# Copying mLSTM scores out of PSUM at once, and loading the low-rank matrices as 128 rows, in a hybrid mixer layer

## The chip, the cores and the metric

The kernel runs on one core of a Trainium2 chip. The metric is the time of one execution on the device in microseconds; lower is better. The core has a matrix engine (TensorE, "PE" in the profile, with its weight loads as "PEld"), three engines for elementwise work (VectorE or DVE, ScalarE or ACT, GpSimd or POOL), a sync engine (SyncE or SP) that issues most transfers, and 16 DMA engines that carry them. Matmuls write to PSUM, a small memory of eight banks of 128 x 512 fp32 numbers; everything else lies in SBUF, 128 partitions wide.

## What is computed

The reference is one layer of a trunk with four parallel token mixers (a convolution module, a bidirectional mLSTM, a bidirectional gated DeltaNet, a bidirectional RWKV-7) on 256 context and 256 latent tokens of width 2048, merged with sigmoid gates, and then a gated convolutional feed-forward. Two places matter here. The mLSTM scan, for each of four heads and two directions:

```python
s = jnp.einsum('ghtd,ghsd->ghts', qt, kt) * dw
num = iw[..., None] * jnp.einsum('ghtd,ghde->ghte', qt, C) + jnp.einsum('ghts,ghse->ghte', s, vt)
den = iw * jnp.einsum('ghtd,ghd->ght', qt, n) + jnp.sum(s, axis=-1)
h = num / jnp.maximum(jnp.abs(den), jnp.exp(-mt))[..., None]
```

and the low-rank decay and learning-rate projections of RWKV-7, of rank 96 plus one bias row:

```python
wl = p['rw_w0'] + jnp.einsum('btr,nrw->btnw', jnp.tanh(xw), p['rw_w2'])
iclr = jax.nn.sigmoid(p['rw_a0'] + jnp.einsum('btr,nrw->btnw', xa, p['rw_a2']))
```

## The kernel before

**Large products.** Every large weight matrix is streamed once. `load_split` (L187 to L200) loads 256 rows as two tiles of 128 rows (`raw`, four buffers, issued by SyncE at L194), makes a rounded high part on ScalarE (`hi`, L198) and the rest on VectorE (`lo`, L199), two buffers each; TensorE then does three products for each block (high by high, high by low, low by high), all at L79. `mode_b_steps` keeps the weights as the stationary operand (`psB`), `mode_a` the tokens (`psA`).

**Order of the work.** The program is written stage by stage: modulation and first projections (`phase0`), the RWKV columns, features and scan, the columns of the other branches, the DeltaNet scan, the mLSTM scan (`ml_scan`), the gate columns (`gates`), the end of the convolution module, the four merges (branches 3, 2, 1, 0), the output projection, the feed-forward. The order in which each engine takes its instructions isn't that of the text: the program is built with `schedule_with_timeline_sim=True`, so a planner simulates it and orders each engine's queue, and matmuls of the gates stand between those of the mLSTM scan. On the chip each engine then works strictly in its queue's order. Tiles get their SBUF addresses from the pools, and a tile that takes over the place of another waits until that one was read for the last time. A generator feeds pieces of the modulation product (`psw`, `psf`) in between.

**The low-rank load.** `rw_open` makes the tile `lora` of 97 partitions, 2 x 2 x 512 numbers each, and `rw_columns` fills it with one transfer (L578) from an input that `layout` puts together on the host (96 rank rows and the bias row). The same function starts the product with `w_mix` (eight loads of 480 KB), whose loads stand behind it in SyncE's queue. `rw_feat` reads `lora` in 32 matmuls (`pslo`).

**The mLSTM scan.** `ml_scan` treats all 512 keys and the 256 latent queries of a head at once. It takes its PSUM banks from a pool of three ("aux"). For each head, eight matmuls write the scores to two banks (`psq0`, `psq1`). Then for each direction d: five matmuls write the row terms of the decay logarithm, with the mask, to one bank (`psr`); ScalarE makes the weights `mA` by exponentials (L1248, L1251, L1253); VectorE multiplies them with the scores in PSUM (L1255, L1256, L1259); fourteen matmuls with the values write numerator and denominator to one bank (`psn`); ScalarE and VectorE normalise into `mlh` (L1267 to L1274). `mA` has two buffers. The masks are drawn by GpSimd in a tile `mlmf` and copied to bf16 by VectorE (L1235), ahead of the heads. After the heads, `head_out` normalises `mlh` over heads and writes the branch's output for its merge.

**The merge.** `merge` loads gate values (`sig`, issued at L1332) and multiplies them with the product of a branch (L1338 for the first merge, L1340 after that).

Of the kernel before, what the change touches and what calls it, by code (L numbers as in the profile page):

```python
# [11 lines left out]
F32 = mybir.dt.float32  # L12
# [8 lines left out]
P = 128  # L21
# [20 lines left out]
class Kern:  # L42
# [499 lines left out]
    def rw_open(self):  # L542
        rp = self.pool("rp2", stack=self.rwx, side="right")
        T = lambda nm, s: rp.tile(s, F32, name=nm)
        self.kT, self.kk = T("kT", [P, 4, 512]), T("kk", [P, 4, 512])
        self.thx, self.xa, self.g32 = T("thx", [97, 512]), T("xa", [97, 512]), T("g32", [32, 512])
        self.rT, self.vL = T("rT", [P, 4, 256]), T("vL", [P, 4, 256])
        self.lora = T("lora", [97, 2, 2, 512])
        self.w2, self.a2 = self.lora[:, 0], self.lora[:, 1]
        self.dv = self.dp.tile([512, 4, P], F32, name="dv")  # L550

    def rw_columns(self):
# [623 lines left out]
    def ml_scan(self):  # L1176
        nc = self.nc
        self.mlx = ExitStack()
        mp = self.pool("mrp", stack=self.mlx)
        wa = self.pool("mwa", bufs=2, stack=self.mlx)  # L1180
        wp = self.pool("mwb", bufs=2, stack=self.mlx)
        qk = self.pool("mqk", stack=self.mlx)
        mqT, mkT = qk.tile([P, 4, 256], F32, name="mqT"), qk.tile([P, 4, 512], F32, name="mkT")
        mv = mp.tile([P, 4, 4, 132], F32, name="mv")
        nc.gpsimd.memset(mv[:, :, :, 128:129], 1.0)
        nc.sync.dma_start(out=mqT, in_=self.dmq)
        nc.sync.dma_start(out=mkT, in_=self.dmk)
        for j in range(4):
            nc.sync.dma_start(out=mv[:, j, :, 0:P], in_=self.dmv[:, j].rearrange("p (h e) -> p h e", h=4))
        e = mp.tile([P, 4, 2, 4], F32, name="mle")  # L1190
        em = mp.tile([P, 2, 2, 4], F32, name="mlem")
        rr = []
        ident = self.ident
        for d in range(2):
            li, lf, b, m = (mp.tile([4, 512], F32, tag="mr%d" % k, name="mr%d" % k) for k in range(4))
            for src, dst in ((self.li, li), (self.lf, lf)):
                ps = self.aux("psml")
                for j in range(4):
                    self.tr(ps[0:4, P * j : P * j + P], src[:, j, d])
                nc.scalar.activation(dst, ps[0:4], AF.Copy)  # L1200
            one = self.ones[0:4, 0:1].to_broadcast([4, 256])
            for seg in range(2):
                v = (lambda ap: ap[:, 0:256] if seg == 0 else ap[:, 256:512])
                f = v if d == 0 else (lambda ap: ap[:, 255::-1] if seg == 0 else ap[:, 511:255:-1])
                pos = 255 if d == 0 else 0
                i0 = (0.0, 0.0) if seg == 0 else (b[:, pos : pos + 1], m[:, pos : pos + 1])
                nc.vector.tensor_tensor_scan(f(b), one, f(lf), i0[0], ALU.mult, ALU.add)
                nc.vector.tensor_tensor_scan(f(m), f(lf), f(li), i0[1], ALU.add, ALU.max)
            nc.vector.tensor_tensor(li, li, b, ALU.subtract)
            ps = self.aux("psmt")  # L1210
            for j in range(4):
                self.tr(ps[:, 4 * j : 4 * j + 4], li[:, P * j : P * j + P])
            for j in range(2):
                self.tr(ps[:, 16 + 4 * j : 20 + 4 * j], m[:, 256 + P * j : 384 + P * j])
            nc.vector.tensor_copy(e[:, :, d], ps[:, 0:16].rearrange("p (j h) -> p j h", h=4))
            nc.scalar.activation(em[:, :, d], ps[:, 16:24].rearrange("p (j h) -> p j h", h=4), AF.Exp, scale=-1.0)
            self.dbg("mlm%d" % d, m)
            self.dbg("mlb%d" % d, b)
            r = mp.tile([4, 256], F32, name="mlr%d" % d)
            nc.vector.tensor_tensor(r, b[:, 256:512], m[:, 256:512], ALU.subtract)  # L1220
            rr.append(r)
        sel = mp.tile([4, 4, P], F32, name="mlsel")
        for h in range(4):
            nc.vector.tensor_copy(sel[:, h], ident[0:4, h : h + 1].to_broadcast([4, P]))
        idb = mp.tile([P, P], BF16, name="idb")
        nc.vector.tensor_copy(idb, ident)

        ms = mp.tile([P, 2, 2, P], BF16, name="mlmask")
        mf = mp.tile([P, P], F32, name="mlmf")
        for d in range(2):  # L1230
            nc.gpsimd.memset(mf, 0.0)
            sg = 1 if d == 0 else -1
            nc.gpsimd.affine_select(out=mf, in_=mf, pattern=[[sg, P]], compare_op=ALU.is_ge, fill=-1e30, base=0, channel_multiplier=-sg)
            for i in range(2):
                nc.vector.tensor_copy(ms[:, d, i], mf)  # L1235
        hs = mp.tile([P, 2, 4, P], F32, name="mlh")
        for h in range(4):
            pq = [self.aux("psq%d" % i) for i in range(2)]
            for j in range(4):
                self.mm(pq[j // 2][:, 256 * (j % 2) : 256 * (j % 2) + 256], mkT[:, h, P * j : P * j + P], mqT[:, h])  # L1240
            for d in range(2):
                pr = self.aux("psr")
                self.mm(pr[:, 0:256], sel[:, h], rr[d])
                self.mm(pr[:, 256:512], sel[:, h], rr[d], start=True, stop=False)
                self.mm(pr[:, 256:512], idb, ms[:, d].rearrange("p i t -> p (i t)"), start=False, stop=True)
                A = wa.tile([P, 4, 256], F32, tag="mA", name="mA")
                for j in range(2):
                    nc.scalar.activation(A[:, j], pr[:, 0:256], AF.Exp, bias=e[:, j, d, h : h + 1])  # L1248
                full = (2, 1) if d == 0 else (3, 0)
                bl = lambda i: slice(P * i, P * i + P)  # L1250
                nc.scalar.activation(A[:, full[0], bl(full[1])], pr[:, bl(full[1])], AF.Exp, bias=e[:, full[0], d, h : h + 1])  # L1251
                for i in range(2):
                    nc.scalar.activation(A[:, 2 + i, bl(i)], pr[:, 256 + P * i : 384 + P * i], AF.Exp, bias=e[:, 2 + i, d, h : h + 1])  # L1253
                A2 = lambda ap: ap.rearrange("p j t -> p (j t)")
                nc.vector.tensor_tensor(A2(A[:, 0:2]), A2(A[:, 0:2]), pq[0], ALU.mult)  # L1255
                nc.vector.tensor_tensor(A[:, full[0]], A[:, full[0]], pq[1][:, 256 * (full[0] - 2) : 256 * (full[0] - 2) + 256], ALU.mult)  # L1256
                o = 5 - full[0]
                ob = bl(o - 2)
                nc.vector.tensor_tensor(A[:, o, ob], A[:, o, ob], pq[1][:, 256 * (o - 2) + ob.start : 256 * (o - 2) + ob.stop], ALU.mult)  # L1259
                pn = self.aux("psn")  # L1260
                for i in range(2):
                    js = [j for j in range(4) if j < 3 or i == 1] if d == 0 else [j for j in range(4) if j != 2 or i == 0]
                    for q, j in enumerate(js):
                        self.mm(pn[:, 132 * i : 132 * i + 129], A[:, j, bl(i)], mv[:, j, h, 0:129], start=q == 0, stop=q == len(js) - 1)
                dn = wp.tile([P, 2, 1], F32, tag="dn", name="dn")
                p3 = pn[:, 0:264].rearrange("p (i c) -> p i c", c=132)
                nc.scalar.activation(dn, p3[:, :, 128:129], AF.Abs)  # L1267
                nc.vector.tensor_tensor(dn, dn, em[:, :, d, h : h + 1], ALU.max)
                nc.vector.reciprocal(dn, dn)
                for i in range(2):  # L1270
                    if d == 0:
                        nc.vector.tensor_scalar(hs[:, i, h], p3[:, i, 0:P], dn[:, i], None, ALU.mult)
                    else:
                        nc.vector.scalar_tensor_tensor(hs[:, i, h], p3[:, i, 0:P], dn[:, i], hs[:, i, h], ALU.mult, ALU.add)  # L1274
        self.dbg("mlh", hs)
        self.head_out(mp, "mh", hs, self.mo, "ml_norm_g", 1)
        self.mlx.close()
# [369 lines left out]
def layout(inputs):  # L1647
# [27 lines left out]
    lora = [np.concatenate([f[w][0].transpose(1, 0, 2), f[b][0][None]], axis=0) for w, b in (("rw_w2", "rw_w0"), ("rw_a2", "rw_a0"))]  # L1675
    r = {n: f[n] for n in ("x", "ctx", "w_mod", "b_mod", "norm_g", "w_in", "rw_g2", "w_br", "w_out", "ffn_up", "ffn_down")}
    r["vec"] = np.concatenate([cols[nm] for nm in VEC], axis=1)
    r["lora"] = np.stack(lora, axis=1)
    r["w_mix"] = np.concatenate([wi[:, C_XW : C_XW + 96], wi[:, C_MLG : C_MLG + 16], wi[:, C_GDG : C_GDG + 16], wi[:, C_XA : C_XA + 352]], axis=1)
    r["taps"] = f["ffn_dw"][0].reshape(396, P).T  # L1680
    return {n: np.ascontiguousarray(a) for n, a in r.items()}
# [18 lines left out]
```

## Time and profile before

| | us |
|---|---|
| three runs | 2306.84, 2308.45, 2312.79 (median 2308.45) |
| profiled execution, its own time | 2311.59 |
| its span, first to last instruction | 2309.5 |
| TensorE busy | 2209.9 |
| VectorE busy | 1446.7 |
| ScalarE busy | 994.1 |
| GpSimd busy | 364.4 |
| mean granted TensorE clock | 0.982 of full speed |

The profile is that of one execution. Busy time is the time in which an engine ran an instruction; the granted clock is the share of TensorE's full speed that the chip allowed at the time. Tiles are named as in the program, without buffer numbers. A wait is put down to the instruction that ended it. A row of the timeline gives start and length in microseconds, engine, line, operation, output and inputs, and in brackets the idle time ahead of it with what ended it.

### The profile page before, as it was taken

The numbers are of one execution on the slowest core, as the hardware profiler recorded it, in microseconds if no ns is written. First come the engines' busy times: TensorE is split into PE (matmuls) and PEld (weight loads), VectorE is DVE, ScalarE is ACT, GpSimd is POOL, SyncE is SP. The second block draws the span as 40 slices with busy tenths as digits, with TensorE's granted clock in tenths as the row PEclk, the third lists the DMA queues.
The fourth block names the chain that finished last, engine by engine and source line by source line (L and its number), as shares of the span: only waits on it lengthen the run. The fifth ranks groups of instructions, "written<-read, shape, count | busy, mean of one in ns | idle before, by whom it ended". The sixth has DMA issues, their size and how long they took to land.

```text
span 2309.5 us, 42812 instructions
## 1 busy us (share of the span) xinstructions
PE 2209.9 (96%) x16828; PEld 1807.2 (78%) x16828; DVE 1446.7 (63%) x3084; ACT 994.1 (43%) x1506; POOL 364.4 (16%) x736
## 2 busy tenths in 40 slices
PE   6979899999999999999999899989999999999998
PEld 3657667877888677677777678779999999998886
DVE  3357766734555698457564486568766677775554
ACT  4225644533444344344245344454333344444443
POOL 0012553533455021010000033000000000000000
PEclk8989999999999999999999899999999999999999
DMA  9934663555665777777786576567777666666663
GB/s 371 361 111 127 171 185 113 161 172 158 198 201 172 242 231 244 235 236 215 215 265 209 172 264 205 174 208 228 229 222 226 210 183 183 176 212 201 194 193 101
DMA packets 273867, 471.97 MB, mean 204 GB/s; under 512 B 41761, under 2 KB 80929, under 8 KB 272673
## 3 DMA queue, kind: packets, MB, share of 16 engines
q1 hardware_dynamic: 273378, 467.14, 65.2%
q8 instruction: 132, 2.16, 0.4%
q10 hardware_dynamic: 288, 2.10, 0.2%
q14 instruction: 69, 0.57, 0.1%
HBM read 440.33 MB, written 28.84 MB: 203 GB/s over the span
## 4 chain that ended last, share of the span: by engine, by line
PE 83%; DVE 7%; DMA 5%; ACT 3%; issue 2%; POOL 1%; SPq 0%; DVEq 0%; ACTq 0%; POOLq 0%
PE psB L79 37%; PE psA L79 21%; PE psD L79 10%; PE psw L79 4%; DVE lo L199 2%; DMA wraw<-in_w_mod 2%; DMA raw<-in_w_mix 1%; PE psG L79 1%; ACT hi L198 1%; DVE cacc L869 1%; PE psf L79 1%; PE psn L79 1%; DMA raw<-in_w_in 1%; PE psSA L79 1%; PE psY L79 0%
## 5 line engine op out<-in xcount | busy, mean ns | idle before, releaser
L199 DVE TENSOR_TENSOR lo<-raw,hi 128x1024 fp32r<-128x1024 f32 (+2 forms) x488 | 600.9, 1233 | 452.9 <-ACT hi L198 443.4
L198 ACT ACTIVATE hi<-raw 128x1024 fp32r<-128x1024 f32 (+2 forms) x488 | 508.4, 1044 | 792.6 <-PE psB L79 347.3
L79 PE MATMUL psB<-u2l,hi 128*128 128x256 f32 x1408 | 396.3, 283 | 0.0
L79 PE MATMUL psB<-u2h,lo 128*128 128x256 f32 x1408 | 395.8, 284 | 0.0
L79 PE MATMUL psB<-u2h,hi 128*128 128x256 f32 x1408 | 394.1, 286 | 0.0
L79 PE MATMUL psA<-lo,uh 128*128 128x512 f32 x832 | 336.7, 405 | 8.9 <-DVE lo L199 8.7
L79 PE MATMUL psA<-hi,ul 128*128 128x512 f32 x832 | 331.1, 398 | 0.0
L79 PE MATMUL psA<-hi,uh 128*128 128x512 f32 x832 | 310.7, 404 | 4.5 <-DVE mg L1338 3.5
L79 PE MATMUL psB<-uh,hi 128*128 128x256 f32 (+1 forms) x832 | 279.7, 344 | 18.6 <-ACT hi L198 16.3
L79 PE MATMUL psB<-ul,hi 128*128 128x256 f32 (+2 forms) x832 | 278.6, 339 | 0.0
L79 PEld LDWEIGHTS psB<-u2h,hi 128*128 128x128 f32 x1408 | 266.9, 192 | 10.4 <-issue 10.3
L79 PE MATMUL psB<-uh,lo 128*128 128x256 f32 (+2 forms) x832 | 263.0, 339 | 8.1 <-DVE lo L199 8.1
L79 PEld LDWEIGHTS psB<-u2l,hi 128*128 128x128 f32 x1408 | 270.7, 192 | 0.0
L79 PEld LDWEIGHTS psB<-u2h,lo 128*128 128x128 f32 x1408 | 269.9, 192 | 0.5 <-issue 0.4
L79 PEld LDWEIGHTS psA<-lo,uh 128*128 128x128 f32 x832 | 157.4, 189 | 59.4 <-DVE lo L199 16.1
L79 PEld LDWEIGHTS psB<-uh,hi 128*128 128x128 f32 x832 | 157.9, 190 | 50.5 <-ACT hi L198 18.4
L79 PEld LDWEIGHTS psA<-hi,uh 128*128 128x128 f32 x832 | 154.6, 190 | 52.9 <-issue 14.1
L79 PEld LDWEIGHTS psA<-hi,ul 128*128 128x128 f32 x832 | 157.3, 189 | 35.7 <-issue 2.0
L79 PEld LDWEIGHTS psB<-uh,lo 128*128 128x128 f32 (+1 forms) x832 | 152.9, 189 | 32.0 <-DVE lo L199 10.6
L79 PEld LDWEIGHTS psB<-ul,hi 128*128 128x128 f32 (+1 forms) x832 | 157.8, 190 | 22.8 <-issue 6.2
L1550 DVE TENSOR_TENSOR lo<-raw,hi 128x1024 fp32r<-128x1024 f32 x88 | 107.6, 1225 | 77.1 <-ACT hi L1549 77.0
L1457 DVE SCALAR_TENSOR_TENSOR facc<-fpad,ffdw,facc 128x256 f32<-128x256 f32 x352 | 151.1, 483 | 0.2
(570 smaller groups left out, 2879.6 us busy)
## 6 DMA issues: line engine op xcount, KB each, us to landing
raw<-in_w_in SPq DMA_DIRECT2D x208, 512.0 KB, 4.5
raw<-in_ffn_up SPq DMA_DIRECT2D x176, 512.0 KB, 3.8
wraw<-in_w_mod SPq DMA_DIRECT2D x160, 512.0 KB, 5.3
raw<-in_ffn_down SPq DMA_DIRECT2D x88, 512.0 KB, 4.4
raw<-in_w_br SPq DMA_DIRECT2D x32, 512.0 KB, 4.8
raw<-in_w_out SPq DMA_DIRECT2D x32, 512.0 KB, 4.7
raw<-in_w_mod SPq DMA_DIRECT2D x32, 512.0 KB, 4.7
raw<-in_w_in SPq DMA_DIRECT2D x48, 256.0 KB, 4.1
```

Of the source, the lines that this page charges most:

```text
L79: self.nc.tensor.matmul(out, lhsT, rhs, start=start, stop=stop)
L198: nc.scalar.activation(hi[s], raw[s], AF.Copy)
L199: nc.vector.tensor_tensor(lo[s], raw[s], hi[s].bitcast(F32), ALU.subtract)
L869: nc.vector.scalar_tensor_tensor(a, cpad[:, i, t : t + 256], w(i, t), a, ALU.mult, ALU.add)
L1457: nc.vector.scalar_tensor_tensor(s3(acc), pad[:, dy : dy + 4, dx : dx + 64], tap(t, b), s3(acc), ALU.mult, ALU.add)
L1550: nc.vector.tensor_tensor(f(lo), f(raw), f(hi).bitcast(F32), ALU.subtract)
```

## The change

Three edits. The tile `lora` gets 128 partitions instead of 97, and the host pads the input with zeros to 128 rows; the matmuls read the first 97 as before. In `ml_scan`, both score banks are copied to an SBUF tile `sc` of one buffer, one by VectorE and one by ScalarE, and the products with the weights read `sc`. The mask is drawn in a corner of the result tile `mlh`, which is made earlier for that, and the tile `mlmf` is gone.

```diff
-        self.lora = T("lora", [97, 2, 2, 512])
-        self.w2, self.a2 = self.lora[:, 0], self.lora[:, 1]
+        self.lora = T("lora", [P, 2, 2, 512])
+        self.w2, self.a2 = self.lora[0:97, 0], self.lora[0:97, 1]
...
-        mf = mp.tile([P, P], F32, name="mlmf")
+        hs = mp.tile([P, 2, 4, P], F32, name="mlh")
+        mf = hs[:, 0, 0]
...
-        hs = mp.tile([P, 2, 4, P], F32, name="mlh")
         for h in range(4):
             pq = [self.aux("psq%d" % i) for i in range(2)]
             for j in range(4):
                 self.mm(pq[j // 2][:, 256 * (j % 2) : 256 * (j % 2) + 256], mkT[:, h, P * j : P * j + P], mqT[:, h])
+
+            sc = mp.tile([P, 2, 512], F32, tag="sc", name="msc")
+            for i in range(2):
+                self.evac(sc[:, i], pq[i], "act" if i else "dve")
+            pq = [sc[:, i] for i in range(2)]
...
-    r["lora"] = np.stack(lora, axis=1)
+
+    r["lora"] = np.pad(np.stack(lora, axis=1), ((0, P - 97), (0, 0), (0, 0), (0, 0)))
```

## The prediction

> **What bounds the kernel now.** The page comes first: who is busy, and where that breaks off.
>
> ```profile
> PE 2209.9 (96%) x16828; PEld 1807.2 (78%) x16828; DVE 1446.7 (63%) x3084; ACT 994.1 (43%) x1506; POOL 364.4 (16%) x736
> PE   6979899999999999999999899989999999999998
> PEclk8989999999999999999999899999999999999999
> PE 83%; DVE 7%; DMA 5%; ACT 3%; issue 2%; POOL 1%; SPq 0%; DVEq 0%; ACTq 0%; POOLq 0%
> ```
>
> TensorE (PE) is busy for 96% of the span, and 83% of the chain that ended last is its work. Work that TensorE covers is free; a microsecond is won only where TensorE stands still or runs at a low clock. Both edits lie beside such places. The granted clock drops to 0.8 in the third slice (115 to 173 us, which holds several small gaps) and again in the 23rd (1270 to 1328); to find the exact stretches I cut the span into stages.
>
> ```profile
> core 0: us, PE busy (x) PEld busy (x) DVE busy (x) ACT busy (x) POOL busy (x), PEclk, DMA share, GB/s
> 161.70:173.20 11.50, 0.00 (x0) 0.00 (x0) 2.68 (x1) 1.00 (x1) 2.62 (x3) 0.61 0.20 64
> 173.20:178.00 4.80, 4.76 (x11) 3.23 (x12) 2.32 (x2) 1.09 (x2) 0.00 (x0) 0.50 0.53 142
> 1207.00:1298.00 91.00, 91.00 (x488) 67.04 (x486) 40.73 (x68) 46.83 (x73) 1.31 (x1) 1.00 0.69 209
> 1298.00:1303.40 5.40, 4.28 (x21) 2.89 (x17) 1.27 (x2) 2.14 (x5) 0.00 (x0) 1.00 0.59 190
> 1303.40:1320.40 17.00, 9.71 (x45) 7.68 (x45) 6.23 (x18) 2.87 (x11) 2.82 (x3) 0.63 0.26 72
> 1320.40:1325.00 4.60, 4.54 (x11) 3.57 (x12) 3.77 (x13) 0.00 (x0) 0.53 (x1) 0.51 0.84 320
> 1360.00:1380.00 20.00, 17.83 (x75) 13.66 (x74) 14.93 (x13) 6.37 (x6) 8.63 (x7) 1.00 1.00 382
> ```
>
> Columns: length, busy time (count) by engine, granted clock, DMA share, GB/s. From 161.7 to 173.2 TensorE does nothing, and it then works 4.8 us at clock 0.50. From 1207 to 1298 it is full at clock 1.00; from 1298 to 1325 it has gaps and a low clock. One hole follows the low-rank load, the other is the end of the mLSTM scan.
>
> **First hole: the low-rank load.** The timeline of SyncE (SPq), the listing of transfers by stretch, and the waits around it:
>
> ```profile
> lora<-in_lora SPq DMA_DIRECT2D x1, 776.0 KB
> 135.83 0.31 SPq L578 DMA_DIRECT2D lora<-in_lora  x1
> 143.88 32.16 SPq L194 DMA_DIRECT2D raw<-in_w_mix  x6
> 135.90:143.80 7.90, 7.90 (x34) 6.40 (x32) 3.94 (x8) 2.26 (x3) 0.27 (x4) 0.93 0.07 23
> raw<-in_w_mix SPq DMA_DIRECT2D x2, 480.0 KB, 28.5
> raw<-in_w_mix SPq DMA_DIRECT2D x8, 480.0 KB, 4.3
> mkT<-dmk SPq DMA_DIRECT2D x1, 1024.0 KB, 7.5
> 172.19 1.00 ACT L198 ACTIVATE hi<-raw 128x960 fp32r<-128x960 f32 x1 [11.20 <-DMA raw<-in_w_mix]
> 173.24 0.79 PE L79 MATMUL psB<-uh,hi 128*128 128x512 f32 x1 [11.59 <-ACT hi L198]
> 178.06 0.39 PE L79 MATMUL psB<-uh,hi 128*128 128x512 f32 x1
> L79 PE MATMUL pslo<-thx,lora x16: 590/592/697, 207.4 to 296.6; 97*128 97x512 f32 x16
> 160.29 0.69 ACT L516 ACTIVATE rwsq<-pskk,eps 128x512 f32<-128x512 f32 x1 [5.93 <-PE pskk L79]
> 161.04 3.34 DVE L517 RECIPROCAL rwsq<-rwsq 128x512 f32<-128x512 f32 x1
> 191.19 1.14 DVE L199 TENSOR_TENSOR lo<-raw,hi 128x960 fp32r<-128x960 f32 x1
> ```
>
> The load of 97 rows goes out at 135.83. Until 143.8 nothing else of weight is moved, and the 16 DMA engines show a share of 0.07 and 23 GB/s: about one of sixteen works. At 23 GB/s 776 KB take 34.5 us, so it ends near 170. The w_mix loads issued from 143.88 on have a share on that same engine, queue behind it there, and land after 28.5 us where their median is 4.3. ScalarE's split (L198) waits 11.20 us for that and TensorE 11.59 us for the split.
>
> With 128 rows the load has the row count of mkT, which is as large (1024 KB) and lands in 7.5 us: it is in by 143.4, ahead of the w_mix loads. Its first reader starts at 207.4, so the extra 248 KB cost nothing; if that cover were gone they would cost 248 KB at 382 GB/s (the rate of the stretch 1360 to 1380), 0.7 us. Then the w_mix data lie ready at about 149. With each queue's order as it is, ScalarE ends its square root at 160.98 and the split at 161.99, 0.3 us after TensorE's last matmul. TensorE then has eight matmuls on the high part and two pskk, which at full clock take half of the 3.6 us that they took at clock 0.50 (173.24 to 176.88), so 1.8 plus start, and is at the low part by 164.3 at the latest; VectorE is in a reciprocal until 164.38 and needs 1.14 us more for the low part, so TensorE waits for 1.2 us. Gain: 11.5 idle, plus half of 4.76 us that ran at clock 0.50, 2.4, less 0.3 and 1.2: **12.4 us**, of which I take 12. What is late next is that reciprocal. Bounds: 14 if the planner moves the low part ahead of it; 9 if the w_mix loads, or VectorE, bring 3 us of new gaps. Everything behind 178 hangs on this chain and moves up with it.
>
> **Second hole: the end of the mLSTM scan.** Timelines of the last head, and the waits of SyncE:
>
> ```profile
> 1295.57 1.89 PE L79 MATMUL psq<-mqT,mkT 128*128 128x256 f32 x8
> 1300.94 1.13 PE L79 MATMUL psr<-mlr,mlsel 4*128 4x256 f32 x4
> 1306.49 2.37 PE L79 MATMUL psn<-mv,mA 128*128 128x129 f32 x14
> 1309.57 0.61 DVE L1272 TENSOR_SCALAR mlh<-psn,dn 128x128 f32<-128x128 f32 x2
> 1310.32 1.17 PE L79 MATMUL psr<-mlr,mlsel 4*128 4x256 f32 x4 [1.47 <-DVE mlh L1272]
> 1313.56 3.35 PE L79 MATMUL psn<-mv,mA 128*128 128x129 f32 x14 [1.75 <-ACT mA L1253]
> 1317.62 0.61 DVE L1274 SCALAR_TENSOR_TENSOR mlh<-psn,dn,mlh 128x128 f32<-128x128 f32 x2
> 1319.73 1.28 DVE L1338 TENSOR_TENSOR mg<-sig,psA 128x512 f32<-128x512 f32 x2
> 1320.46 0.79 PE L79 MATMUL psA<-hi,uh 128*128 128x512 f32 x1 [3.55 <-DVE mg L1338]
> SPq L1332 <- DVE mlh L1274: 9.0, 1, 9.0
> 1207.94 1.99 PE L79 MATMUL psq<-mqT,mkT 128*128 128x256 f32 x8
> L1255 DVE TENSOR_TENSOR mA<-mA,psq 128x512 f32<-128x512 f32 x8 | 5.5, 687 | 12.3 <-ACT mA L1248 12.3
> L382 DVE TENSOR_TENSOR ul<-tmp,uh 128x512 fp32r<-128x512 f32 x16 | 10.7, 689 | 0.4
> L538 ACT ACTIVATE rwvt<-psvT 128x512 f32<-128x512 f32 x2 | 1.2, 600 | 6.5 <-PE psvT L90 6.5
> ```
>
> The auxiliary PSUM pool has three banks here. The scores (psq) hold two until the second direction's last product, so psr and psn of both directions take turns on the third: psr, exponentials, products, psn, normalisation, and only then the next psr, whose matmul waits 1.47 us for the write of mlh at L1272. That is eight half-heads in a row, from 1207.94 to 1318.23: 110.3 us, 13.8 each. While TensorE has gate matmuls in between, this costs nothing. At 1298 it is out of them: the merge behind it fills its banks, its sig loads (L1332) wait 9.0 us for the last mlh, and its first eviction (L1338) stands behind the scan in VectorE's queue at 1319.73.
>
> The copies free both score banks at once, so the two directions no longer alternate on one bank. Added: four VectorE and four ScalarE copies. The trace has no such VectorE copy; the nearest rows are a product of that size out of PSUM, 0.69 us (L1255), and ScalarE's copy, 0.60 (L538); I take 0.69. A lower end of nothing, or a gain, would need products that get cheaper when they read SBUF, and one that does so takes 0.69 too (L382). That makes 2.8 us on VectorE and 2.4 us on ScalarE, hidden: they are busy for 40.7 and 46.8 of the 91 us. Uncovered they would cost 0.7 us a head in the chain, 2.8 us. The copy target has one buffer, so the copies of one head wait for the products of the one before (L1259); behind them on ScalarE and VectorE stand the splits of the gate weights, on which TensorE feeds. The third edit, the mask drawn in a corner of mlh, swaps one tile for another before any head: nothing.
>
> How much is won does not depend on how much shorter the scan gets, once it ends before TensorE runs out of other work: that needs 110 us to become about 90, and two directions in flight should bring it to 60 to 85. Then the hole closes: idle 1.1 (1298 to 1303.4), 7.3 (1303.4 to 1320.4), and clock losses of 0.37 x 9.71 = 3.6 and 0.49 x 4.54 = 2.2, **14.2 us** in all. I take 11, since the merge moves up against the stretch 1360 to 1380, where the DMA share is 1.00 and TensorE idles 2.2 us already, and since the order will leave some gap. Bounds: 14.2 and zero (below zero is the third rival).
>
> A rule on the clock bears on both sums: the page "TensorE: Matmul & The Clock Gate" of the Trainium skill (Part 1, on the gate) says that full rate returns after about 3.4 us of steady work, so a restart would cost about 1.7 us, an estimate from that figure. The trace shows 4.8 us at 0.50 behind the first hole, longer than the page has it; with 1.7 for the first restart and 3.4 for the second hole's two, the sum below would be about 3 us smaller.
>
> **Sum.** 12 and 11 make 23 us. The profiled execution took 2311.6 us (span 2309.5 and 2.1 around it) and would come to 2288.6; it lies 3.1 above the median of the three runs, 2308.45, so the forecast for the median is 2285.5, rounded to 2286.
>
> **Rivals.** *Only the load pays.* The order of every queue comes from a planner that simulates the program; it may leave the end of the scan where it is, by placing the scan's matmuls among the gates as sparsely as now (the gap from psn's end to the next psr is often its choice, not a wait), or the merge may find another reason to wait. For it: the scan's waits total little up to 1298. Against: the bank is a true wait in the last head. Price: 2308.45 - 12 = 2296.5. The page "TensorE: Matmul & The Clock Gate" of the Trainium skill (section on HAM oscillation) tells of a kernel kept busy by its loop order, to which more PSUM buffers gave nothing; that is this rival, and no run here shows it yet.
>
> *The load does not get shorter*, or another load holds the w_mix loads up as long. For it only that no transfer into this tile with 128 rows is in the trace; against it mkT and every w_mix load, all of 128 rows. Price: only the scan, 2308.45 - 11 = 2297.5.
>
> *The single copy buffer stalls the splits.* ScalarE works in order. If the planner puts the next head's copy early, it blocks until the previous head's last product, at worst one half-head, 13.8 us; with it the weight splits block. TensorE has two split buffers ahead, each good for 12 matmuls at 0.19 us (91.00 us over 488), 4.5 us together; beyond that it starves: 9.3 us at each of three handoffs, plus a cold restart of 2.4 each, 35 us. With the scan's gain lost, 2308.45 - 12 + 35 = 2331. It decides from a block of about 6 us per handoff (4.5, and 12 / 3 less the restart). Against it: the planner simulates such waits, and VectorE and ScalarE are only half busy.
>
> *Both gains are given back* by a new order or new SBUF addresses elsewhere (the mLSTM pool grows by 3.5 KB per partition, 4 for the copies less 0.5 for the mask, and the tiles after it move): within 7 us of before.
>
> **How the numbers follow.** About 0.3%, 7 us, is what a measurement of this kernel can tell from no change. Chances: both holes close 0.56; only the load 0.24; only the scan 0.07; given back 0.08; the stall 0.05. The first three are faster by over 0.3%: 0.87. Same 0.08, slower 0.05. Low end: both at their upper bounds, 14 + 14.2, give 2280, and a new order may bring the 7 more that the fourth rival allows it: 2273. High end: only the load, at its lower bound of 9: 2300. A range of 2280 to 2291 would be that of the likeliest case alone.
>
> **What the profile after would show.** Right: the lora load lands in about 7 us; no w_mix load takes over 10; no idle TensorE stretch at 160 to 175; in the scan psr of the second direction starts before psn of the first is read out; psq of the next head follows within some 20 us; the scan ends at least 15 us ahead of where gate and merge matmuls run out, and the clock stays at 1.00 there. Wrong: w_mix landings near 28 us; a scan of 110 us; ScalarE waiting for L1259 ahead of a copy while TensorE waits for splits; a lasting gap where the merge starts.

## The result and the profile after

The changed kernel takes 2283.78 us (median of four runs, 2281.39 to 2288.49) against 2310.12 before (2306.84 to 2312.79; median of four, one run more than stood ahead of the forecast): a ratio of 0.9881, with an interval of 0.9863 to 0.9898. It is 26 us faster. The forecast was 2286. The profiled execution took 2285.63 us, 26.0 less than that of before.

The page of the changed kernel, the same lines as before:

```profile
PE 2203.7 (96%) x16828; PEld 1802.0 (79%) x16828; DVE 1447.1 (63%) x3088; ACT 997.0 (44%) x1511; POOL 368.4 (16%) x736
PE   5999899999999999999999999989999999999998
PEclk8999899999999999999999999999999999999999
PE 83%; DVE 7%; DMA 4%; ACT 3%; issue 2%; POOL 1%; SPq 0%; DVEq 0%; POOLq 0%; ACTq 0%
```

TensorE has the same 16828 matmuls; 6 us less busy time for the same work fits less of it running at a low clock. The clock row has lost the dips at 115 to 173 us and at the end of the mLSTM scan. Besides the first slice, the fifth (228 to 285) is now at 0.8. It holds gaps that the kernel before has as well (PE row, same place), and in a second profile of the changed kernel that slice is at 0.9, so it differs from one execution to the next.

**The first hole.** Of the eight w_mix loads two go out ahead of the lora load and six behind it, in both kernels; the hole hung on those behind. Rows from the timeline of the changed kernel (start, duration, and in brackets the wait ahead of it):

```profile
137.52 0.34 SPq L578 DMA_DIRECT2D lora<-in_lora  x1
...
163.59 0.50 PE L79 MATMUL psB<-uh,hi 128*128 128x512 f32 x1 [0.28 <-ACT hi L198]
162.69 3.34 DVE L517 RECIPROCAL rwsq<-rwsq 128x512 f32<-128x512 f32 x1
165.96 3.25 DVE L199 TENSOR_TENSOR lo<-raw,hi 128x960 fp32r<-128x960 f32 x2
167.10 0.50 PE L79 MATMUL psB<-uh,lo 128*128 128x512 f32 x1 [0.98 <-DVE lo L199]
```

Its transfers, with the median from issue to landing at the end:

```profile
lora<-in_lora SPq DMA_DIRECT2D x1, 1024.0 KB, 4.8
raw<-in_w_mix SPq DMA_DIRECT2D x8, 480.0 KB, 3.6
```

And the group that reads the load (first and last start behind the durations):

```profile
L79 PE MATMUL pslo<-thx,lora x16: 590/592/697, 196.7 to 288.3; 97*128 97x512 f32 x16
```

The load of 1024 KB lands in 4.8 us, where the one of 776 KB had taken about 34.5 by the estimate from its 23 GB/s. The eight w_mix loads have a median of 3.6; the two issued first behind the lora load land in 4.0, against 28.5 before. Of the 11.59 us in which TensorE waited for ScalarE's split, 0.28 are left, and then 0.98 for the low part, which starts at 165.96 because VectorE's reciprocal ends there. From the issue of the load to its first reader it is now 196.7 - 137.5 = 59.2 us, against 207.4 - 135.8 = 71.6 before: **12.4 us** won.

**The second hole.** Rows from the timeline: the scores of the first three heads (psq), the second head up to the write of its first direction, and the scan's last write:

```profile
1197.77 1.99 PE L79 MATMUL psq<-mqT,mkT 128*128 128x256 f32 x8
1217.62 1.89 PE L79 MATMUL psq<-mqT,mkT 128*128 128x256 f32 x8
1223.91 1.13 PE L79 MATMUL psr<-mlr,mlsel 4*128 4x256 f32 x4
1228.86 0.61 PE L79 MATMUL psn<-mv,mA 128*128 128x129 f32 x4
1229.40 1.13 PE L79 MATMUL psr<-mlr,mlsel 4*128 4x256 f32 x4
1233.66 0.61 DVE L1277 TENSOR_SCALAR mlh<-psn,dn 128x128 f32<-128x128 f32 x2
1238.28 1.89 PE L79 MATMUL psq<-mqT,mkT 128*128 128x256 f32 x8
1282.69 0.61 DVE L1279 SCALAR_TENSOR_TENSOR mlh<-psn,dn,mlh 128x128 f32<-128x128 f32 x2
```

The groups of the copies and of the products that read them:

```profile
L94 ACT ACTIVATE msc<-psq x4: 597/597/597, 1199.8 to 1260.8; 128x512 f32<-128x512 f32 x4
L96 DVE COPY msc<-psq x4: 672/680/682, 1199.8 to 1260.2; 128x512 f32<-128x512 f32 x4
L1260 DVE TENSOR_TENSOR mA<-mA,msc x8: 683/693/695, 1205.0 to 1274.8; 128x512 f32<-128x512 f32 x8
```

The row terms (psr) of the second direction go out at 1229.40, while the value matmuls (psn) of the first have barely begun and 4 us before these are read out (L1277). Before, they had to wait for that. The second head's scores start at 1217.62 and the third's at 1238.28; a head takes about 21 us instead of 27.6, and the scan 85.5 us (1197.77 to 1283.3) instead of 110.3. To see what that was worth, take the stretch from the first psq to the first eviction of the output projection, by stages; the columns are length, busy time of PE, PEld, DVE, ACT and POOL, granted clock, DMA share and GB/s. Before:

```profile
1207.94:1436.90 228.96, 215.99 (x1034) 166.92 (x1033) 134.15 (x201) 103.13 (x161) 43.45 (x28) 0.96 0.67 213
```

After, with the start of the merge in a row of its own:

```profile
1197.80:1411.00 213.20, 209.87 (x1032) 162.44 (x1032) 133.39 (x204) 106.00 (x166) 46.14 (x28) 1.00 0.71 229
1290.00:1340.00 50.00, 46.70 (x202) 36.49 (x201) 39.64 (x62) 24.38 (x34) 10.89 (x7) 1.00 0.82 283
```

It shrank from 228.96 to 213.20 us, by **15.8**: TensorE's idle time in it fell from 12.97 to 3.33 us, and its busy time from 215.99 to 209.87, all of it now at clock 1.00. What is left, 3.3 us, lies at the start of the merge.

### The profile page after: what moved, and what is told of

Same layout as the page of the kernel before. It is cut to its first block, busy times and chain, and to the rows that moved or that the text cites. A ratio compares the mean times of both kernels' runs of the same rounds, so it can differ in the third digit from the quotient of the medians.

```text
span 2283.8 us, 42818 instructions
## 1 busy us (share of the span) xinstructions
PE 2203.7 (96%) x16828; PEld 1802.0 (79%) x16828; DVE 1447.1 (63%) x3088; ACT 997.0 (44%) x1511; POOL 368.4 (16%) x736
## 4 chain that ended last, share of the span: by engine, by line
PE 83%; DVE 7%; DMA 4%; ACT 3%; issue 2%; POOL 1%; SPq 0%; DVEq 0%; POOLq 0%; ACTq 0%
PE psB L79 38%; PE psA L79 21%; PE psD L79 10%; PE psw L79 4%; DMA wraw<-in_w_mod 3%; DVE lo L199 2%; PE psG L79 1%; DVE cacc L869 1%; ACT hi L198 1%; PE psf L79 1%; PE psn L79 1%; PE psSA L79 1%; PE psY L79 1%; PE pd L79 0%; PE psR L79 0%
## 5 line engine op out<-in xcount | busy, mean ns | idle before, releaser
L199 DVE TENSOR_TENSOR lo<-raw,hi 128x1024 fp32r<-128x1024 f32 (+2 forms) x488 | 599.5, 1230 | 434.5 <-ACT hi L198 420.8
```

The lines of the kernel that those rows point to most:

```text
L199: nc.vector.tensor_tensor(lo[s], raw[s], hi[s].bitcast(F32), ALU.subtract)
```

## The experiments

One table carries most of them: lengths in us, in the profiled execution of each, and the ratio of its time to that of the kernel before on the same chip. "Load" is from the issue of the lora load to its first reader, "scan" from the first psq to the end of the last write of mlh, "stage" from the first psq to the first eviction of the output projection. Between the first reader of lora and the first psq the program is the same but for where the mask is drawn, and that part took 996 to 1004 us in these profiles; so the totals of single runs differ by several us for no cause of their own, and the stages tell more.

| kernel | load | scan | stage | ratio to before |
|---|---|---|---|---|
| before | 71.6 | 110.3 | 229.0 | 1 |
| changed | 59.2 | 85.5 | 213.2 | 0.9881 (0.9863 to 0.9898) |
| changed, run again | 60.6 | 85.4 | 213.4 | 0.9889 (0.9872 to 0.9905) |
| only the load as 128 rows | 59.2 | 110.1 | 229.4 | 0.9944 (0.9929 to 0.9959) |
| only the copies | 71.9 | 86.4 | 214.5 | 0.9929 (0.9913 to 0.9946) |
| 106 rows | 59.2 | 110.2 | 229.2 | 0.9938 (0.9923 to 0.9953) |
| 97 rows from ScalarE's queue | 59.7 | 110.3 | 229.1 | 0.9952 (0.9935 to 0.9969) |
| one bank copied | 59.2 | 85.9 | 213.3 | 0.9894 (0.9877 to 0.9910) |
| copied twice | 59.2 | 85.4 | 212.0 | 0.9895 (0.9879 to 0.9911) |
| one buffer for mA | 59.4 | 93.5 | 219.0 | 0.9921 (0.9906 to 0.9937) |
| copied, but banks held | 59.1 | 108.0 | 227.0 | 0.9956 (0.9941 to 0.9970) |
| both psr first | 59.1 | 69.4 | 218.3 | 0.9908 (0.9893 to 0.9923) |

The theory at this point: two holes, each closed by one edit; the first by spreading a load over more DMA engines, the second by ending the scan before TensorE runs out of other work. The rivals: the gains hang together; one of them comes from a new order of the queues and not from its named cause; the copies themselves cost or gain something.

### Only the load as 128 rows

```diff
-        self.lora = T("lora", [97, 2, 2, 512])
+        self.lora = T("lora", [P, 2, 2, 512])
...
-    r["lora"] = np.stack(lora, axis=1)
+    r["lora"] = np.pad(np.stack(lora, axis=1), ((0, P - 97), (0, 0), (0, 0), (0, 0)))
```

> Only the load as 128 rows; the scan as before. Theory: the 97-row load sits on one of the sixteen DMA engines for 34.5 us and the w_mix loads queue behind it; with 128 rows the first hole closes and nothing else changes, so 12.3 us less than before (2297.8 against a median of 2310.1; 9 to 14 less), first reader of lora about 12 us earlier, the scan still 110 us long. Rival, that the shift is given back further down: less than 5 us are left at the end.

Measured: 2299.85 us against 2313.58 on the same chip, 13.7 less, ratio 0.9944. The load part is 59.2 us, as in the full change; scan and stage are those of before. The queues of all engines are those of before, but for this one transfer, so the gain is the load's own and nothing of it is given back.

### Only the copies

The changed kernel with the tile `lora` of 97 rows again.

> Only the score copies (and the mask in the corner of mlh); the load as before with 97 rows. Theory: the scan ends some 25 us earlier, the hole at its end closes and the merge has fewer gaps, so 15.8 us less than before, as landmarks of the two traces give it (14 to 17). Rival, that the two edits only pay together (a shift in the first stage was needed to line up the loads of the merge): under 12 us.

Measured: 2298.69 us against 2313.58, 14.9 less, ratio 0.9929. The load part is that of before (71.9), the stage 214.5. The two ratios multiply to 0.9944 x 0.9929 = 0.9873, within the interval of the whole change: the edits add up. The rival that they need each other falls.

### 106 rows: how many engines a load gets

```diff
-        self.lora = T("lora", [P, 2, 2, 512])
+        self.lora = T("lora", [106, 2, 2, 512])
```

with the padding to 106 rows.

> The load as 106 rows (97 and nine of zeros), scan as before. This tells how the row count sets the number of DMA engines. The trace gives 23 to 26 GB/s for one engine. If the number of engines is the largest one up to sixteen that divides the row count, 106 = 2 x 53 gives two engines: 848 KB at about 50 GB/s land in 17 us, at about 154, before TensorE needs the w_mix data at 161.7, so the time is that of the 128-row version within 1.5 us though the load is three times slower. This is the rule that the page DMA: Bandwidth & Descriptors of the Trainium skill states (section on why a DMA increments its semaphore by 16). Rival, only multiples of sixteen are spread: one engine, 36 us, and the time of before or up to 1 us more.

The stretch while only this load runs, in the stages of this kernel:

```profile
141.00:147.00 6.00, 6.00 (x27) 4.87 (x27) 2.33 (x5) 1.69 (x2) 0.13 (x2) 0.98 0.13 52
```

A DMA share of 0.13 and 52 GB/s, where the 97-row load showed 0.07 and 23: two engines of sixteen. The load takes about 17 us (an estimate: 848 KB at 52 GB/s), and the time is that of 128 rows (0.9938 and 0.9944, intervals almost the same). The first two w_mix loads behind it still take 14.8 us, to about 162, and ScalarE's split of them starts at 164.02 without a wait for them: the cover just holds. So the count of engines follows from the row count, and not from whether it is a multiple of sixteen.

The page "DMA: Bandwidth & Descriptors" of the Trainium skill (section on why a DMA increments its semaphore by 16) says that a transfer gets the largest number of engines, up to 16, that divides its slowest dimension. The rows agree with it: one engine for 97 rows, two for 106, and the 128-row load had landed 4.8 us after its issue.

### The 97-row load from another queue

```diff
-        nc.sync.dma_start(out=self.lora, in_=A["lora"])
+        nc.scalar.dma_start(out=self.lora, in_=A["lora"])
```

> The load with 97 rows as before, but issued from ScalarE's queue instead of SyncE's; scan as before. Theory A, the w_mix loads wait in the order of one queue on the one busy engine: from another queue the two share that engine, the w_mix loads land in under 10 us and the time is 11 to 13 less than before, though the load itself still takes over 30 us. Theory B, the engine itself is the limit whatever the queue: w_mix landings stay above 20 us and the time is within 3 us of before.

The stages of this kernel while the load runs alone:

```profile
138.50:146.00 7.50, 7.50 (x35) 6.15 (x34) 3.74 (x7) 1.69 (x2) 0.27 (x4) 1.00 0.07 25
```

ScalarE's queue (q10) in the stretch from 143 to 180, with packets and MB:

```profile
q10 hardware_dynamic: 87, 0.70, 5.1%
```

The two w_mix loads issued first behind it, still on SyncE's queue:

```profile
raw<-in_w_mix SPq DMA_DIRECT2D x2, 480.0 KB, 15.1
```

The load still runs alone at 25 GB/s and is still under way past 143 (0.70 MB on its queue after that). These two w_mix loads land in 15.1 us: not the 28.5 that the same two took before, and not the 4.0 beside the spread load either. So it is the order within one queue that made them wait for all of the slow load. The 11 us that are left over the 4.0 fit two queues that take turns on the one engine; that was not traced engine by engine. The load part is 59.7 us, half a microsecond off the spread load, and the time is 11.2 us under that of before (2302.39 against 2313.58). Theory A holds, but for the landing, which I had put under 10; ScalarE's splits still wait for w_mix data, 10.1 us in three waits, but TensorE's wait for the split stays at 0.28. Against the 128-row version the difference of 2.5 us in the medians is inside both intervals.

### One bank copied

```diff
-            for i in range(2):
-                self.evac(sc[:, i], pq[i], "act" if i else "dve")
-            pq = [sc[:, i] for i in range(2)]
+            self.evac(sc[:, 1], pq[1], "act")
+            pq = [pq[0], sc[:, 1]]
```

> The changed kernel with only the second score bank copied (by ScalarE); the first stays held until the second direction's products. Theory: what counts is that the scan's eight half-heads no longer take turns on one bank, and the gain is full once the scan ends before TensorE runs out of gate work; with two banks the two directions can alternate, the scan takes 85 to 95 us instead of 85.5, and the time is that of the changed kernel or up to 3 us more (0.9881 to 0.9895 of before). Rival, both banks have to be free, since the next head needs two of them: scan over 100 us, 10 us or more slower than the changed kernel (over 0.9925 of before).

Measured: ratio 0.9894, stage 213.3, scan 85.9. One freed bank does all that two do. The rival falls: what the scan lacked was a second bank beside psr's, so that the directions need not alternate.

### Each bank copied twice

```diff
-            for i in range(2):
+            for i in (0, 1, 0, 1):
```

> The changed kernel with each score bank copied twice to the same tile. Theory: the copies lie under TensorE's work, so 2.7 us more on VectorE and 2.4 us more on ScalarE cost less than 1.5 us (ratio to before 0.9875 to 0.9890). Rival, the copies lie on the chain of the scan and that chain sets the end: 0.7 us a head, 2.8 us or more.

Measured: ratio 0.9895, against 0.9881 and 0.9889 of the changed kernel. By the ratios that is 3.2 or 1.4 us more (0.0014 or 0.0006 of 2310), just above what was expected and well inside the intervals, so by the times it can be told neither from zero nor from the rival's 2.8. The stage shows it more sharply: it took 212.0 us, not longer than 213.2, and the scan 85.4. Four more copies on each engine are hidden.

### One buffer for the weights mA

```diff
-        wa = self.pool("mwa", bufs=2, stack=self.mlx)
+        wa = self.pool("mwa", bufs=1, stack=self.mlx)
```

> The changed kernel with one buffer for the weights mA instead of two, so that the exponentials of one direction wait for the value matmuls of the other. Theory: overlap of the two directions is what shortens the scan; without it the scan goes back to 95 to 110 us, and 3 to 14 us of the gain are lost. Rival, the gain comes from the earlier scores of the next head alone: scan below 90 us and no loss over 1.5 us.

Measured: ratio 0.9921, scan 93.5 us, stage 219.0. The scan is 8 us longer and the stage 5.8. A scan of 95 to 110 us was expected; it is 93.5, so most of the shortening, 17 of 25 us, stays without the second buffer. The rival's scan below 90 us with no loss falls as well. The stages where the merge starts:

```profile
1290.00:1300.00 10.00, 6.69 (x32) 5.18 (x28) 7.45 (x17) 2.50 (x3) 3.35 (x3) 1.00 0.56 169
1300.00:1320.00 20.00, 18.49 (x80) 15.29 (x81) 16.19 (x30) 8.78 (x14) 0.00 (x0) 0.91 0.73 242
1320.00:1340.00 20.00, 17.73 (x74) 13.36 (x73) 17.44 (x22) 11.25 (x17) 7.29 (x6) 1.00 0.70 249
```

The hole is back in small: 3.3 us idle right behind the scan, 1.5 and 2.3 after that, and a clock of 0.91. Freed banks alone bring the stage from 229.0 to 219.0; the last 5.8 us need the second mA too. With a scan of 93.5 us TensorE still runs out of other work before the merge.

### Copies made, banks held

The changed kernel without the line `pq = [sc[:, i] for i in range(2)]`: the copies are made, nothing reads them, and the products read PSUM until the second direction is done.

> The changed kernel with both banks copied, but the products read the scores in PSUM as before, so the copies are made and free nothing. Theory: the copies by themselves gain nothing and cost nothing, the scan takes 110 us again, and the time is that of the version with only the 128-row load (0.994 of before, within 1.5 us). Rival, the gain came from a new order or from products that read SBUF: at or below 0.990.

Measured: ratio 0.9956, scan 108.0, stage 227.0. That is the version with only the load (0.9944, 110.1, 229.4) within the intervals, though by the ratios 2.8 us above it, where at most 1.5 was expected. So the copies by themselves gain nothing, and neither does the mask in the corner of mlh, which this kernel has too. That the gain isn't in products that read SBUF shows elsewhere: they take 693 ns against 688 from PSUM, and with one bank copied the largest of them still read PSUM. What is left is the freed bank, together with the order that the planner makes of it: in the traces, 32 of TensorE's 16828 matmuls stand in another place here than in the load-only version, and 671 in the changed kernel than in the one before. No kernel has the freed bank in the old order, so the two can't be told apart.

### Row terms of both directions first

```diff
+            prs = []
             for d in range(2):
                 pr = self.aux("psr")
...
+                prs.append(pr)
+            for d in range(2):
+                pr = prs[d]
                 A = wa.tile([P, 4, 256], F32, tag="mA", name="mA")
```

> The changed kernel with the row terms (psr) of both directions written ahead of either direction's products, so that both can be in flight on two banks. Is anything left in the scan? The changed kernel still has 3.3 us of idle TensorE at the start of the merge (1290 to 1340). Theory: the scan gets shorter, 65 to 80 us instead of 85.5, and the time falls by 1 to 3.3 us at most. Rival, the chain's length no longer matters at all: within 1 us of the changed kernel; or holding two banks for psr keeps the next head's scores waiting, and the scan gets longer.

The changed kernel itself was run again beside it:

> The changed kernel itself, on the same chip as the one above, for comparison: 0.988 of before, as on record (0.9863 to 0.9898).

The scan gets shorter, 69.4 us, and yet the kernel is not faster: 0.9908, against 0.9889 for the changed kernel on the same chip (2291.49 and 2286.43 us). The intervals of the ratios overlap; the stages, 218.3 against 213.4 us, do show a loss. Neither theory nor rival had that. The stages of the scan's middle and of the start of the merge:

```profile
1230.00:1270.00 40.00, 40.00 (x215) 30.33 (x214) 18.95 (x39) 19.08 (x37) 3.38 (x3) 0.96 0.56 164
1300.00:1304.00 4.00, 1.13 (x5) 0.58 (x4) 4.00 (x6) 2.80 (x3) 1.37 (x1) 1.00 0.93 283
1304.00:1308.00 4.00, 0.24 (x1) 0.27 (x2) 3.55 (x8) 2.84 (x8) 0.00 (x0) 0.64 0.92 325
```

Its timeline on SyncE's queue, VectorE and TensorE:

```profile
1287.31 12.08 SPq L194 DMA_DIRECT2D raw<-in_w_br  x4
1299.48 1.37 SPq L1341 DMA_DIRECT2D sig<-dg  x3
1306.94 0.68 DVE L1347 TENSOR_TENSOR mg<-sig,psA 128x512 f32<-128x512 f32 x1
1307.76 0.77 PE L79 MATMUL psA<-hi,uh 128*128 128x512 f32 x1 [6.63 <-DVE mg L1347]
```

The same places in the changed kernel:

```profile
1287.93 6.17 SPq L194 DMA_DIRECT2D raw<-in_w_br  x3
1294.15 1.46 SPq L1337 DMA_DIRECT2D sig<-dg  x3
1300.82 1.28 DVE L1343 TENSOR_TENSOR mg<-sig,psA 128x512 f32<-128x512 f32 x2
```

The scan is done at 1265.7, but the merge's first gate values (sig) go out only at 1299.48, behind a run of four weight loads that occupy SyncE's queue for 12.08 us. In the changed kernel they go out at 1294.15, behind three that take 6.17. In both, VectorE's first product with them starts some 7 us later (1306.94 and 1300.82), and TensorE, which stands for that product's eviction, has lost 6.63 us and the clock has fallen to 0.64. The chain of work in this trace runs the same way: the third of the gate loads lands 6.19 us after it was issued, at 1306.61, and the product follows at 1306.94. A smaller part of the loss lies in the scan itself: from 1230 to 1270 TensorE has no gap and yet a clock of 0.96, which is 0.04 x 40 = 1.6 us; why it fell there is open. So beyond a certain point the scan no longer sets when the merge starts. What sets it here is the place of the gate loads in SyncE's queue, as these rows have it; but no kernel with only that place changed was run, and how the planner came to its order was not tried.

## Why the prediction was right

**The load.** 12.4 us worked out, 12.4 measured. Its steps hold one by one: one engine of sixteen (and two with 106 rows), w_mix loads behind it in the queue, the split within 0.3 us of TensorE's last matmul (0.28), then the reciprocal as what is late next (a wait of 1.2 forecast, 0.98 measured). The landing was put at 7.5 us and was 4.8, which changes nothing, as it was hidden either way.

**The scan.** The mechanism was right: the held bank made the directions alternate, psr of the second direction now overtakes the reading of the first, 85.5 us lie just above the forecast 60 to 85, and the next head follows after 21. The size was off: 11 taken, 15.8 measured, above the upper bound of 14.2. The step that failed is the last one, "I take 11, since the merge moves up against the stretch 1360 to 1380". I had the hole of 1298 to 1325 (8.4 idle, 5.8 clock) and expected the merge behind it to idle more. It idles less: of 12.97 us idle in the whole stage, 8.5 lay in the hole and 4.5 behind it, in the merge, and 3.33 are left in all. The clock's part was sized well: 5.8 forecast, 6.1 us less busy time measured. Which part of that comes from loads that now have more time between scan and merge was not tried by itself.

**"How much is won does not depend on how much shorter the scan gets."** Half right. The point from which the gain is full was put at a scan of about 90 us, and 93.5 us falls short of it by 5.8. But beyond it the time is not indifferent: with 69.4 us the stage is 5 us longer again, for what looks like another reason.

**The copies.** Prices as taken: 0.68 us on VectorE, 0.60 on ScalarE, products 0.69 from either memory; hidden, as the doubled copies show.

**The rivals.** "Only the load pays" falls with the version that has only the copies. The rule that the prediction named there, from the page "TensorE: Matmul & The Clock Gate" of the Trainium skill (section on HAM oscillation), is about a kernel to which more PSUM buffers gave nothing; here freed banks gave 15.8 us, because TensorE did run dry at the end of the scan. "The load does not get shorter" with the one that has only the load. The stall by the single copy buffer did not occur: among ScalarE's waits in the changed kernel's scan, those ahead of the copies are for psq alone, 5.5 us in four.

```profile
ACT msc L94 <- PE psq L79: 5.5, 4, 1.6
```

"Both are given back" falls with the stages behind: from the first eviction of the output projection to the last store it is 869 us, before as after.

**The sum.** 12 and 11 were forecast between the two profiled executions, 26.0 came: 12.4 and 15.8, less 1.7 that the first stage took longer ahead of the load and 0.6 between the two places, both within what single runs differ by. That the median was missed by only 2.2 us is in part luck: the gain was missed by 3.3 (23 forecast, 26.3 measured), and the forecast started from 2308.45, which with the fourth run became 2310.12.

## What to carry to other kernels

Look at the DMA share while a single load runs: a share near one sixteenth, like the 0.07 here, says that one engine carries it, and what stands behind it in the same queue pays. Here 97 rows did that; padded rows (106 or 128) or another queue gave the time back. When a scan with long turnaround shares a full TensorE with other work, count the PSUM banks that it holds across its inner loop; one bank freed by a copy can be worth more than the copy costs, but only until the scan ends before the other work does, and after that other waits decide.

## What the runs showed of the hardware

At a DMA share of 0.07, one engine of sixteen, a load moved 23 to 25 GB/s; at 0.13, two engines, 52. The same two loads of 480 KB landed in 28.5 us behind the slow load in its own queue, in 15.1 with the slow load on another queue, where I had expected under 10, and in 4.0 with the load spread over 128 rows.

A shorter scan made its stage longer: at 69.4 us of scan the stage took 218.3 us, at 85.5 us it took 213.2, with the next stage's gate loads later in one queue. In that scan the granted clock fell to 0.96 over 40 us in which TensorE had no gap.
